# Sixty-eight elementwise operations moved from GpSimd to VectorE, and new figures in the planner that lays out a decoder layer

## The chip, the cores and the metric

The kernel runs on one core of one Trainium2 chip. A core has five engines with a queue of instructions each: TensorE (PE in the profile; PEld is its weight load), VectorE (DVE), ScalarE (ACT), GpSimd (POOL) and SyncE (SP, which here issues all DMAs). The metric is the device time of one execution in microseconds (us); the time before is the median of three runs.

## The reference

The reference computes one decoder layer in float32 for a sequence of 2048 tokens of width 1024. The input is normed and projected once to 59 blocks of 128 columns; the projection is cut into three branches, each of which has its own gate:

```python
h = rms_norm(x, norm_g[l])
p = h @ w_in[l]
y_a = rwkv7_mix(p_r, p_k, p_v, p_w, p_a, ...) * jax.nn.silu(z_a)
y_b = sliding_window_sink_attn(p_q, p_sk, p_sv, positions, ...) * jax.nn.silu(z_b)
y_c = memory_cross_attn(p_xq, mem, ...) * jax.nn.silu(z_c)
merged = (gates[:, :, 0] * (y_a @ w_proj_a[l]) + gates[:, :, 1] * (y_b @ w_proj_b[l])
          + gates[:, :, 2] * (y_c @ w_proj_c[l]))
x = x + (merged @ w_out[l])
```

Branch A is a recurrence over time with a state of 64x64 for each of 8 heads (`rwkv7_scan`). Branch B is attention over a sliding window of 128 tokens, branch C attention into 256 memory tokens.

## The kernel before

**Tiling.** The sequence is worked in four blocks of 512 tokens (`sb` from 0 to 3 in `build`). Within a block, features stand on the 128 partitions and the 512 tokens along the free axis.

**Dense products.** A float32 operand is cut into a high and a low part (type float32r), and a dense product is three matmuls, high by high, high by low and low by high (`gemm3`, L401, L402, L403; in the output projection L1036, L1037, L1038). The high part is a copy on ScalarE, the low part a subtraction. For the outputs of the branches this is `split_y`: ScalarE's copy at L829, the subtraction at L830, on GpSimd. It runs 48 times, 12 in each block of tokens. The keys of the memory are split in the same way at L547 (4 times).

**Weight blocks.** `wblock` brings 128 rows by 512 columns of a weight. In the first block of tokens it loads the raw block (tile `wraw`, L382), makes the high part on ScalarE (L383) and the low part on VectorE (L384) in a tile `whl`, and stores `whl` to memory (L387, tiles `k`). In the later three blocks it loads `whl` from there (L379). There are three buffers of each.

**The recurrence.** `rwkv_pair` works a pair of heads in 8 chunks of 64 tokens, one after the other. A chunk is a chain between TensorE and VectorE of three links: two matmuls at L749 give a product that VectorE copies to `W` (L760); two at L767 read `W`, and VectorE copies the result into `Z` (L773, L774); two at L777 read `Z`, and VectorE makes the next state (L784, twice), which L749 of the next chunk reads. There are 16 pairs, so 128 chunks. At L652, on GpSimd, r is multiplied by k for the bonus term, once for each pair. L678 to L680 are a loop of 31 steps on VectorE that inverts small triangles ahead of the chain. TensorE fills the time between links with dense matmuls of other branches.

**The other branches.** `swa_pair` (window attention) scales probabilities on VectorE (L983), transposes them on TensorE (L987), copies them on ScalarE (L989) and multiplies them by the values (L992). `merge` multiplies the branches by their output weights and gates (L1003, L1015, L1018, L1019).

**What sets the order.** The program is written by generators that are woven together, and then laid out anew. `steps` makes one step of each instruction, with the steps it depends on, a cost (`cost_PE`, `cost_DVE` and so on: how long the engine is busy, and when the result is there) and a rank, its number in the program. `lay_out` then goes through a clock of its own: for each engine it keeps the steps whose inputs are there by its reckoning, takes the engine that can start first, and on it the ready step of lowest rank (on TensorE with a preference for staying in one tile shape). A result of another engine is seen `LAT` ns after its reckoned end. A step that opens a tile waits until a buffer of that tag is free; buffers go in program order. `order` nails the result down as the order of every engine's queue. The small roots and powers of the norms (`rpow`, L366 to L370) stay on GpSimd in both kernels.

Of the kernel before, what the change touches and what calls it, by code (L numbers as in the profile page):

```python
# [9 lines left out]
F32 = mybir.dt.float32  # L10
# [4 lines left out]
ALU = mybir.AluOpType  # L15
# [24 lines left out]

LAT = {"PE": 55, "DVE": 45, "ACT": 35, "POOL": 80, "SP": 30}
NAMES = {mybir.EngineType.PE: "PE", mybir.EngineType.DVE: "DVE", mybir.EngineType.Activation: "ACT",
         mybir.EngineType.Pool: "POOL", mybir.EngineType.SP: "SP"}

# [1 line left out]
class Step:  # L48
# [32 lines left out]
    def cost_PE(self):  # L81
        out, mov, w = self.writes[0], *self.reads[:2]
        n = self.n(out)
        self.tile = tuple(128 if r[3][0][1] > 64 else 64 if r[3][0][1] > 32 else 32 for r in (mov, out))
        self.dense = mov[5] == F32R
        if self.dense:
            self.busy = 12 + 0.424 * n
        elif self.ins.is_transpose:
            self.busy = 108 if self.tile[0] == 128 else 55
        elif self.tile[1] == 128:  # L90
            self.busy = 223 + max(0, n - 128) * 1.7 if self.tile[0] == 128 else 223 + max(0, n - 128) * 0.8
        else:
            self.busy = max(58, 0.86 * n)
        self.dur = self.busy + 160

    def cost_ACT(self):
        r = self.reads[0]
# [13 lines left out]
        self.busy = self.dur + 80  # L111

    def cost_SP(self):
        self.dur, self.busy = 3300, 330


def steps(instructions, manual):

    out, masks, seen, byname, opener = [], {}, {}, {}, {}
    for ins in instructions:  # L120
        if isinstance(ins, mybir.BassTilePoolBoundary):
            continue
        s = Step(ins, masks)
        for rs, w in ((s.reads, False), (s.writes, True)):
            for name, parts, words, _, psum, _ in rs:
                s.before |= {q for q, w2, p2, m2 in seen.get(name, ()) if (w or w2 or psum) and q is not s and p2 & parts and m2 & words}
        for name, parts, words, *_ in s.reads:
            seen.setdefault(name, []).append((s, False, parts, words))
        for name, parts, words, *_ in s.writes:
            old = seen.setdefault(name, [])  # L130
            old[:] = [x for x in old if x[0] is s or x[2] & ~parts or x[3] & ~words] + [(s, True, parts, words)]
        s.before |= {byname[x] for x in manual.get(ins.name, ())}
        s.before |= {opener.setdefault(r[0], s) for r in s.writes + s.reads} - {s}
        for b in s.before:
            b.after.append(s)
        byname[ins.name] = s
        s.rank = len(out)
        out.append(s)
    return out

# [8 lines left out]
def lay_out(tc, todo):  # L149

    metas = {tag: meta.bufs for p in tc.info.pools if p.space != bass.MemoryType.DRAM for tag, meta in p.tag_meta.items()}
    source = {t.name: t.source_name for t in tc.info.tiles}
    tags = {tag: Tag(b) for tag, b in metas.items()}
    users, opened = {}, set()
    for s in todo:
        for name in {r[0] for r in s.reads + s.writes}:
            users.setdefault(name, []).append(s)
        for r in s.writes:
            if source[r[0]] in tags and r[0] not in opened:
                opened.add(r[0])  # L160
                s.opens.append(r[0])
                tags[source[r[0]]].queue.append(r[0])
    left = {name: len(u) for name, u in users.items()}
    heads = {tag: 0 for tag in tags}
    clock = {e: 0.0 for e in NAMES.values()}
    ready, parked = {e: {} for e in clock}, set()
    orders = {e: [] for e in clock}
    missing = {s: len(s.before) for s in todo}

    def seen_by(s, b):  # L170

        if b.eng == s.eng:
            return 0 if s.eng == "PE" else b.end + 30
        return b.end + LAT[s.eng]

    def room(s):

        at = 0.0
        for name in s.opens:
            t = tags[source[name]]  # L180
            if t.queue[heads[source[name]]] != name or not t.free:
                return None
            old = t.free[0]
            if old:
                at = max([at] + [seen_by(s, b) for b in last[old].values()])
        return at

    def offer(s):
        at = room(s)
        if at is None:  # L190
            parked.add(s)
            ready[s.eng].pop(s, None)
        else:
            parked.discard(s)
            ready[s.eng][s] = max([at] + [seen_by(s, b) for b in s.before])

    last = {name: {} for name in users}
    for s in todo:
        if not missing[s]:
            offer(s)  # L200
    tile, fp32 = (128, 128), False
    for _ in todo:
        best = None
        for e, rs in ready.items():
            if rs:
                at = max(clock[e], min(rs.values()))
                if best is None or at < best[0]:
                    best = at, e
        at, e = best
        can = [s for s, t in ready[e].items() if t <= at]  # L210
        s = min(can, key=lambda s: s.rank)
        if e == "PE":
            if tile != (128, 128) and s.tile != tile:
                s = min(can, key=lambda s: (s.tile != tile, s.rank))
            if s.tile != tile:
                at += 95
            if s.dense and fp32:
                clock[e] = at + 95
            else:
                clock[e] = at  # L220
            tile, fp32 = s.tile, not s.dense
            clock[e] += s.busy
        else:
            clock[e] = at + s.busy
        s.end = at + s.dur
        del ready[e][s]
        orders[e].append(s)
        again = set()
        for name in s.opens:
            tag = source[name]  # L230
            tags[tag].free.pop(0)
            heads[tag] += 1
            again.add(tag)
        for name in {r[0] for r in s.reads + s.writes}:
            if e not in last[name] or last[name][e].end < s.end:
                last[name][e] = s
            left[name] -= 1
            if not left[name] and source[name] in tags:
                tags[source[name]].free.append(name)
                again.add(source[name])  # L240
        for a in s.after:
            missing[a] -= 1
            if not missing[a]:
                offer(a)
        if again:
            for a in [a for rs in (parked, *ready.values()) for a in rs if any(source[n] in again for n in a.opens)]:
                offer(a)
    return orders
# [11 lines left out]
def build(tc, A, nsb=4):  # L260
    nc = tc.nc
    es = ExitStack()
    V, S, G, PE = nc.vector, nc.scalar, nc.gpsimd, nc.tensor
# [24 lines left out]
    def s_ps():  # L288
        return ps.tile([128, 512], F32, name="as_", bufs=2)
# [4 lines left out]
    manual = {}  # L294
# [158 lines left out]
    def bcast_T(out, st, nh, ntile):  # L453

        w = 128 // nh
        for i in range(ntile):
            rep = xp.tile([128, nh, w], F32, name="rep", bufs=2)
            V.tensor_copy(rep, st[:, i * nh:(i + 1) * nh].unsqueeze(2).to_broadcast([128, nh, w]))
            PE.transpose(out[:, i * 128:(i + 1) * 128], rep.rearrange("p a b -> p (a b)"), ident)
# [50 lines left out]
    KmH = cp.tile([128, 4, M], F32R, name="KmH")  # L510
    KmL = cp.tile([128, 4, M], F32R, name="KmL")
# [5 lines left out]
    def mem_kv():  # L517
# [23 lines left out]
        def scaled(h):  # L541
            kg = kgs[h][1]
            bc = s_ps()
            bcast_T(bc, sts[h], 1, 2)
            V.tensor_tensor(kg, kg, bc[:, :M], op=ALU.mult)
            S.activation(KmH[:, h], kg, AF.Copy)
            G.tensor_tensor(KmL[:, h], kg, KmH[:, h].bitcast(F32), op=ALU.subtract)  # L547

        o = [o_ps(), s_ps()]
        for h in range(6):  # L550
# [49 lines left out]
    def rwkv_pair(p, sb, hT, lwla, yas):  # L600
        kp = proj(B_K + p, hT)
        k = shift(kp, B_K + p, pcol("mu_k", p), dcol("omu_k", p), sb, "rk_")
# [46 lines left out]
        r = shift(rpj, B_R + p, pcol("mu_r", p), dcol("omu_r", p), sb, "rr_")  # L649
        for Q, h in ((QE, EV), (QO, OD)):  # L650
            V.tensor_tensor(Q[h, :, C:], chunks(r)[h], Pt[h, :, 1:], op=ALU.mult)
        G.tensor_tensor(r, r, k, op=ALU.mult)  # L652

        yield 12

# [19 lines left out]
        for s in range(31):  # L675
            n = 31 - s
# [68 lines left out]
        for c in range(NC_):  # L745
# [15 lines left out]
            SP = rp.tile([128, C], F32, name="SP", bufs=2)  # L761
# [64 lines left out]
    def split_y(y, yh, yl, br, j, sb):  # L826
        a = yp.tile([128, TB], F32R, name="yh")
        b = yp.tile([128, TB], F32R, name="yl")
        S.activation(a, y, AF.Copy)  # L829
        G.tensor_tensor(b, y, a.bitcast(F32), op=ALU.subtract)  # L830
        yh.append(a)
        yl.append(b)

# [346 lines left out]
```

## Time and profile before

| | us |
|---|---|
| median of 3 runs (2529.36 to 2537.97) | 2534.09 |
| the profiled execution | 2550.03 |
| its span, first to last instruction | 2548.2 |
| PE busy in the span | 2450.9 |
| DVE busy | 1546.8 |
| ACT busy | 893.2 |
| POOL busy | 202.2 |

The profile is of one execution. "Idle before" and the view of waits tell how long an engine stood with nothing running and whose event ended it; a wait of PEld is one of the weight load, which runs ahead of the matmul and may stand idle while PE works. The granted clock is the share of full speed that TensorE got; it is 1.0 or 0.5 in each stretch of the record. The times of one float32 matmul are those of two passes in the record, and an ordinary float32 matmul counts as two records.

### The profile page before, as it was taken

How to read it: one execution, taken by the hardware profiler on the slowest of the kernel's cores; microseconds unless marked ns; L12 is line 12 of the kernel's file. 1: busy time of each engine (PE TensorE's matmuls, PEld its weight loads, DVE VectorE, ACT ScalarE, POOL GpSimd, SP SyncE). 2: the span in 40 equal slices, each digit the busy share in tenths (PEclk: the TensorE clock that was granted, in tenths of full speed). 3: DMA queues.
4: the chain of work that ended last, by engine and by line, in shares of the span. 5: the costliest groups of instructions: out<-in, count | busy, mean ns of one | idle time of the engine just before them, and what ended most of it. 6: DMA issues, size and time to landing. Idle time of an engine off the chain costs nothing.

```text
span 2548.2 us, 39384 instructions
## 1 busy us (share of the span) xinstructions
PE 2450.9 (96%) x14496; PEld 1877.5 (74%) x14496; DVE 1546.8 (61%) x4962; ACT 893.2 (35%) x1957; POOL 202.2 (8%) x220
## 2 busy tenths in 40 slices
PE   6999999899999999999999999999999999999999
PEld 5676767678877777677777777767777777777777
DVE  6778876843666956636437685744553777573632
ACT  5445544433324343412223443331231334342120
POOL 1111101100001100100001100010000110000000
PEclk8899999999999999999999999989999999999999
DMA  5344446468842434244573333425466333433546
GB/s 172 133 167 154 171 164 221 159 230 291 304 163 93 150 109 140 93 161 157 178 248 124 104 124 125 149 83 174 141 220 210 100 135 118 141 116 130 176 136 228
DMA packets 132527, 407.37 MB, mean 160 GB/s; under 512 B 15344, under 2 KB 15728, under 8 KB 132336
## 3 DMA queue, kind: packets, MB, share of 16 engines
q1 hardware_dynamic: 132336, 404.86, 46.9%
q8 instruction: 115, 1.88, 0.3%
q14 instruction: 76, 0.62, 0.1%
HBM read 313.58 MB, written 91.23 MB: 159 GB/s over the span
## 4 chain that ended last, share of the span: by engine, by line
PE 73%; DVE 13%; DMA 6%; ACT 5%; issue 2%; SPq 1%; POOL 0%; DVEq 0%; ACTq 0%
PE mm L401 18%; PE mm L403 18%; PE mm L402 17%; DMA whl<-k 3%; PE oo L992 1%; PE rw L777 1%; PE rw L749 1%; PE rw L767 1%; PE oo L881 1%; DVE whl L384 1%; PE rw L662 1%; DVE g L983 1%; ACT g L972 1%; DVE ibc L678 1%; PE mm L1036 1%
## 5 line engine op out<-in xcount | busy, mean ns | idle before, releaser
L401 PE MATMUL mm<-hH,whl 128*128 128x512 f32 x1888 | 773.6, 410 | 13.6 <-DMA whl<-k 10.8
L403 PE MATMUL mm<-hH,whl 128*128 128x512 f32 x1888 | 766.1, 406 | 6.2 <-DVE whl L384 6.0
L402 PE MATMUL mm<-hL,whl 128*128 128x512 f32 x1888 | 762.7, 404 | 0.0
L401 PEld LDWEIGHTS mm<-hH,whl 128*128 128x128 f32 x1888 | 359.8, 191 | 103.4 <-issue 12.5
L403 PEld LDWEIGHTS mm<-hH,whl 128*128 128x128 f32 x1888 | 359.5, 190 | 84.0 <-DVE whl L384 7.6
L402 PEld LDWEIGHTS mm<-hL,whl 128*128 128x128 f32 x1888 | 360.0, 191 | 70.8 <-issue 1.4
L384 DVE TENSOR_TENSOR whl<-wraw,whl 128x512 fp32r<-128x512 f32 x174 | 123.7, 712 | 90.6 <-ACT whl L383 89.8
L383 ACT ACTIVATE whl<-wraw 128x512 fp32r<-128x512 f32 x174 | 109.0, 628 | 149.6 <-PE mm L403 86.5
L763 ACT ACTIVATE SP<-Z,Pt 64x64 f32<-64x64 f32 x256 | 88.5, 346 | 193.3 <-DVE Z L784 189.6
L679 DVE TENSOR_TENSOR ibc<-ibc,Yi 128x248 f32<-128x248 f32 (+30 forms) x496 | 150.4, 303 | 7.5
L1003 ACT ACTIVATE g<-mm 128x512 f32<-128x512 f32 x96 | 57.2, 596 | 273.6 <-PE mm L403 273.4
L401 PE MATMUL mm<-yh,whl 128*128 128x512 f32 x384 | 150.9, 393 | 2.2 <-DVE carry L590 2.2
L678 DVE STREAM_SHUFFLE ibc<-Nc 128x248 f32<-128x248 f32 (+30 forms) x496 | 151.7, 310 | 0.0
L402 PE MATMUL mm<-yl,whl 128*128 128x512 f32 x384 | 150.5, 392 | 0.0
L403 PE MATMUL mm<-yh,whl 128*128 128x512 f32 x384 | 150.2, 391 | 0.0
L680 DVE TENSOR_TENSOR Yi<-Yi,ibc 128x248 f32<-128x248 f32 (+30 forms) x496 | 149.1, 301 | 0.8
L1018 DVE SCALAR_TENSOR_TENSOR g<-g,mm 128x512 f32<-128x512 f32 x64 | 43.9, 685 | 124.9 <-PE mm L403 103.8
L784 DVE SCALAR_TENSOR_TENSOR Z<-rw,Pt,SP 64x64 f32<-64x64 f32 x224 | 63.4, 283 | 59.4 <-PE rw L777 55.6
L972 ACT ACTIVATE g<-g,mxs,st 128x256 f32<-128x256 f32 (+1 forms) x128 | 74.4, 583 | 61.5 <-DVE mxs L965 61.4
L760 DVE COPY W<-rw 128x64 f32<-128x64 f32 x128 | 28.6, 223 | 110.1 <-PE rw L749 109.7
L401 PEld LDWEIGHTS mm<-yh,whl 128*128 128x128 f32 x384 | 72.5, 189 | 17.6 <-DVE carry L590 2.4
L402 PEld LDWEIGHTS mm<-yl,whl 128*128 128x128 f32 x384 | 72.5, 189 | 14.9
(1737 smaller groups left out, 3979.1 us busy)
## 6 DMA issues: line engine op xcount, KB each, us to landing
whl<-k SPq DMA_DIRECT2D x474, 512.0 KB, 3.3
k<-whl SPq DMA_DIRECT2D x158, 512.0 KB, 3.2
wraw<-in_w_in SPq DMA_DIRECT2D x118, 256.0 KB, 3.8
g<-in_x SPq DMA_DIRECT2D x36, 256.0 KB, 5.5
out<-g SPq DMA_DIRECT2D x32, 256.0 KB, 3.5
rt<-in_x SPq DMA_DIRECT2D x28, 256.0 KB, 4.6
wraw<-in_w_proj SPq DMA_DIRECT2D x24, 256.0 KB, 3.5
wraw<-in_w_out SPq DMA_DIRECT2D x16, 256.0 KB, 4.1
```

What stands on the lines that cost most here:

```text
L383: S.activation(w[:, 0], raw, AF.Copy)
L384: V.tensor_tensor(w[:, 1], raw, w[:, 0].bitcast(F32), op=ALU.subtract)
L401: PE.matmul(out, lh, rh, start=i == 0, stop=False)
L402: PE.matmul(out, lh, rl, start=False, stop=False)
L403: PE.matmul(out, ll, rh, start=False, stop=i == n - 1)
L678: V.stream_shuffle(bc[:, :, :n], Nc[:, :, s + 1:], [s] * 32)
L679: V.tensor_tensor(bc[:, :, :n], bc[:, :, :n], Y[:, :, s:s + 1].to_broadcast([128, NC_, n]), op=ALU.mult)
L680: V.tensor_tensor(Y[:, :, s + 1:], Y[:, :, s + 1:], bc[:, :, :n], op=ALU.add)
L763: S.activation(SP[h], Z[h, e, c], AF.Copy, scale=Pt[h, c, C:C + 1])
L784: upd = V.scalar_tensor_tensor(to, pS[h], Pt[h, c, C:C + 1], SP[h], op0=ALU.mult, op1=ALU.add)
L972: S.activation(prs[b][:, i, m0:], prs[b][:, i, m0:], AF.Exp, scale=r2[:, b, i:i + 1], bias=mx[:, b, i:i + 1], accum_out=mx[:, b, 2 + i:3 + i])
L1003: S.activation(t, gp, AF.Tanh, scale=0.5)
```

## The change

Three kinds of lines change. First, the 48 subtractions of `split_y`, the 4 of the memory keys and the 16 products of r and k are given to VectorE. Second, the planner's figures: results of TensorE are seen by other engines 200 ns after their end instead of 55, a matmul's own result takes at least 270 ns, a dense matmul is 2 ns longer, some float32 shapes are costed otherwise, the clock of TensorE is advanced differently where shapes change, and a DMA takes 3800 ns instead of 3300. Third, every step that writes a tile `whl` or `wraw` (the loads of weights, the copy L383 and the subtraction L384) gets a rank that is 1000 lower, so that among ready steps of an engine it is taken before others.

```diff
-LAT = {"PE": 55, "DVE": 45, "ACT": 35, "POOL": 80, "SP": 30}
+LAT = {"PE": 200, "DVE": 45, "ACT": 35, "POOL": 80, "SP": 30}
...
-            self.busy = 12 + 0.424 * n
+            self.busy = 14 + 0.424 * n
...
-            self.busy = 223 + max(0, n - 128) * 1.7 if self.tile[0] == 128 else 223 + max(0, n - 128) * 0.8
+            self.busy = 223 + max(0, n - 128) * 1.7 if self.tile[0] == 128 else 175 + max(0, n - 128) * 0.9
...
-        self.dur = self.busy + 160
+        self.dur = max(270, self.busy + 160)
...
-        self.dur, self.busy = 3300, 330
-
-
-def steps(instructions, manual):
+        self.dur, self.busy = 3800, 380
+
+
+def steps(instructions, manual, ahead=1000):
...
-        s.rank = len(out)
+        s.rank = len(out) - ahead * any(n.startswith(a) for n, *_ in s.writes for a in ("whl", "wraw"))
...
+            clock[e] = at + s.busy
             if s.dense and fp32:
-                clock[e] = at + 95
-            else:
-                clock[e] = at
+                clock[e] += 95
+            elif s.tile != tile and s.tile[1] < 128:
+                clock[e] += 49
             tile, fp32 = s.tile, not s.dense
-            clock[e] += s.busy
...
-            G.tensor_tensor(KmL[:, h], kg, KmH[:, h].bitcast(F32), op=ALU.subtract)
+            V.tensor_tensor(KmL[:, h], kg, KmH[:, h].bitcast(F32), op=ALU.subtract)
...
-        G.tensor_tensor(r, r, k, op=ALU.mult)
+        V.tensor_tensor(r, r, k, op=ALU.mult)
...
-        G.tensor_tensor(b, y, a.bitcast(F32), op=ALU.subtract)
+        V.tensor_tensor(b, y, a.bitcast(F32), op=ALU.subtract)
```

The first place is on TensorE, in one chunk of the recurrence in the second block of tokens. The rows go from L749 to L777; rows of `mm` are dense matmuls, the numbers behind names are those of buffers. Before:

```order
L749 MATMUL rw_11717<-Z_11608,QE_11057 64x64
L749 MATMUL rw_11717<-Z_11608,QO_11058 64x64
L756 MATMUL yps_11672<-Z_11608,QE_11057 64x64
L756 MATMUL yps_11672<-Z_11608,QO_11058 64x64
L402 MATMUL mm_11739<-hL_6530,whl_11742 128x512
L767 MATMUL rw_11727<-W_11722,Tt_156 64x64 x2
L737 MATMUL yps_11672<-Z_11608,AB_11203 64x64 x2
L403 MATMUL mm_11739<-hH_6529,whl_11742 128x512
L401 MATMUL mm_11739<-hH_6529,whl_11742 128x512
L777 MATMUL rw_11734<-Z_11608,bkT_11561 64x64 x2
```

And with the change:

```order
L749 MATMUL rw_11717<-Z_11608,QE_11057 64x64
L749 MATMUL rw_11717<-Z_11608,QO_11058 64x64
L756 MATMUL yps_11672<-Z_11608,QE_11057 64x64
L756 MATMUL yps_11672<-Z_11608,QO_11058 64x64
L402 MATMUL mm_11739<-hL_6530,whl_11742 128x512
L403 MATMUL mm_11739<-hH_6529,whl_11742 128x512
L767 MATMUL rw_11727<-W_11722,Tt_156 64x64 x2
L737 MATMUL yps_11672<-Z_11608,AB_11203 64x64 x2
L401 MATMUL mm_11739<-hH_6529,whl_11742 128x512
L402 MATMUL mm_11739<-hL_6530,whl_11742 128x512
L403 MATMUL mm_11739<-hH_6529,whl_11742 128x512
L777 MATMUL rw_11734<-Z_11608,bkT_11561 64x64 x2
```

Two dense matmuls instead of one stand between L749 and L767, and three instead of two between L767 and L777. Over the 128 chunks the commonest number goes from one (92 chunks) to two (87) in the first of these links, from two (79) to three (73) in the second, and from three (51 of 112) to four (66) between L777 and the next L749. The dense matmuls are the same in number; the changes from a run of dense matmuls to float32 ones and back go from 702 runs to 719.

The second place is on VectorE, in the middle of the second block of tokens, where the probabilities of one head pair are scaled (L983) while the recurrence of another goes on. Before:

```order
L976 RECIPROCAL dns_10497<-dns_10497 128x8
L983 TENSOR_SCALAR g2_10393<-g2_10393,dns_10497 128x256 x2
L983 TENSOR_SCALAR g2_10394<-g2_10394,dns_10497 128x256 x2
L983 TENSOR_SCALAR g2_10409<-g2_10409,dns_10497 128x256 x2
L983 TENSOR_SCALAR g2_10410<-g2_10410,dns_10497 128x256 x2
L1015 SCALAR_TENSOR_TENSOR mB_10493<-g2_10478,mm_10480 128x512
L760 COPY W_10516<-rw_10511 128x64
```

With the change:

```order
L983 TENSOR_SCALAR g2_10409<-g2_10409,dns_10497 128x256 x2
L983 TENSOR_SCALAR g2_10410<-g2_10410,dns_10497 128x256 x2
L830 TENSOR_TENSOR yl_9117<-g2_9112,yh_9116 128x512
L830 TENSOR_TENSOR yl_9620<-g2_9615,yh_9619 128x512
L830 TENSOR_TENSOR yl_10145<-g2_10140,yh_10144 128x512
L1015 SCALAR_TENSOR_TENSOR mB_10493<-g2_10478,mm_10480 128x512
L760 COPY W_10516<-rw_10511 128x64
```

Three of the moved subtractions now stand between the scaling and the copy to `W`. On TensorE, three dense matmuls now stand between the transposes L987 and the L767 that reads this `W`; before, none did. Of the 68 moved operations, 14 have a step of the recurrence among the next three rows of VectorE's queue.

The third place is SyncE's queue in the first block of tokens. Before:

```order
L387 DMA k120_6056<-whl_6051 128x1024
L382 DMA wraw_6100<-in_w_in 128x512
L387 DMA k121_6063<-whl_6058 128x1024
L382 DMA wraw_6134<-in_w_in 128x512
L387 DMA k122_6097<-whl_6092 128x1024
```

With the change:

```order
L382 DMA wraw_6100<-in_w_in 128x512
L387 DMA k120_6056<-whl_6051 128x1024
L382 DMA wraw_6134<-in_w_in 128x512
L387 DMA k121_6063<-whl_6058 128x1024
L382 DMA wraw_6141<-in_w_in 128x512
```

The load of a raw block now stands ahead of the store of an earlier finished one, instead of behind it. At the program's start the first three raw blocks stand ahead of the rows of x, on SyncE as on ScalarE and VectorE; before, they stood behind them.

## The prediction

> **What bounds the kernel now.** I read the page's busy times first, then the waits of PE, of PEld, then the granted clock, then timelines of places where PE stood.
>
> ```profile
> PE 2450.9 (96%) x14496; PEld 1877.5 (74%) x14496; DVE 1546.8 (61%) x4962; ACT 893.2 (35%) x1957; POOL 202.2 (8%) x220
> PE rw L432 <- DVE rt L427: 16.1, 4, 13.9
> PE mm L401 <- DMA whl<-k: 10.8, 12, 2.5
> PE rw L767 <- DVE W L760: 9.2, 6, 2.6
> PE mm L403 <- DVE whl L384: 6.0, 2, 5.3
> PE mm L1036 <- DMA whl<-k: 3.5, 5, 1.0
> PEld rw L777 <- issue: 42.8, 102, 1.6
> PEld rw L767 <- DVE W L760: 33.8, 91, 2.8
> core 0: 2548.2 us, clock 0.979
> ```
>
> TensorE sets the time: it is busy 2450.9 of 2548.2 us, and the change neither adds nor removes a matmul. What can move is the idle 97.3 us, the waits that the busy time hides (a matmul's modelled end covers the short ones), and the clock: a mean of 0.979 means that 0.021 x 2548.2 = 53.5 us were lost at half speed. The first wait of 13.9 us is the start, before the first row of x is normed.
>
> The second thing to see is a place in which three engines stand in each other's way. Here is VectorE, then GpSimd, then TensorE, in the second block of tokens:
>
> ```profile
> 1051.61 5.25 DVE L983 TENSOR_SCALAR g<-g,dns 128x256 f32<-128x256 f32 x8
> 1056.89 0.69 DVE L1015 SCALAR_TENSOR_TENSOR mB<-g,mm 128x512 f32<-128x512 f32 x1
> 1057.50 0.22 DVE L760 COPY W<-rw 128x64 f32<-128x64 f32 x1
> 1052.61 3.84 POOL L830 TENSOR_TENSOR yl<-g,yh 128x512 fp32r<-128x512 f32 x3 [14.44 <-ACT yh L829]
> 1054.70 0.49 PE L987 MATMUL as__10571<-c_ident,g 128*128 128x128 f32 x3
> 1057.77 0.37 PE L767 MATMUL rw<-W,Tt 64*64 64x64 f32 x2 [2.58 <-DVE W L760]
> L983 DVE TENSOR_SCALAR g<-g,dns x128: 268/345/1428, 305.1 to 2287.5; 128x256 f32<-128x256 f32 x120, 128x128 f32<-128x128 f32 x8
> 463.72 1.50 DVE L679 TENSOR_TENSOR ibc<-ibc,Yi 128x208 f32<-128x208 f32 x1
> 463.09 0.36 DVE L680 TENSOR_TENSOR Yi<-Yi,ibc 128x216 f32<-128x216 f32 x1
> ```
>
> Eight scalings take 5.25 us, though the median of one is 345 ns, so 2.8 us for eight; the extra 2.5 us fall exactly where GpSimd runs three subtractions (3.84 us). VectorE is held up by GpSimd's long operations: a product at 463.72 takes 1.50 us where its larger neighbour took 0.36. `W` comes late, and TensorE stands 2.58 us. What follows is worse than the wait. Stretches of the granted clock:
>
> ```profile
> 471.00:481.30 10.30, 9.21 (x22) 6.76 (x23) 8.16 (x40) 5.79 (x19) 0.00 (x0) 0.52 0.62 229
> 1058.00:1068.20 10.20, 10.20 (x83) 7.17 (x79) 2.38 (x10) 3.17 (x7) 0.29 (x1) 0.51 0.01 2
> 1676.00:1696.50 20.50, 20.50 (x114) 13.54 (x114) 3.88 (x16) 3.90 (x10) 0.00 (x0) 0.51 0.07 26
> 2290.00:2303.70 13.70, 13.70 (x93) 8.63 (x89) 3.22 (x13) 3.27 (x8) 0.00 (x0) 0.50 0.00 1
> sum 75.10, PE 73.03 PEld 51.32 DVE 29.79 ACT 16.95 POOL 2.79; mean PE 8.11 PEld 5.70 DVE 3.31 ACT 1.88 POOL 0.31
> ```
>
> The seventh figure behind the stretch's length is the clock. The stretch at 471 follows the 5.3 us wait of L403, the other three follow the same place in the second, third and fourth block of tokens. The sum is over the nine half-clock stretches after the first 300 us.
>
> **The change, term by term.** All gains are TensorE time, since nothing else sets the end.
>
> *Moved operations.* GpSimd loses these, and VectorE gets them at the price of like operations of its own (both inputs in on-chip memory, 128x512):
>
> ```profile
> 0.00:2548.20 2548.20, 63.44 (x48) 0.98 0.47 160
> 0.00:2548.20 2548.20, 21.84 (x16) 0.98 0.47 160
> L1027 DVE TENSOR_TENSOR mB<-mB,g 128x512 fp32r<-128x512 f32 x32 | 22.1, 691 | 16.4 <-ACT g L1025 16.1
> L633 DVE TENSOR_TENSOR rt<-rt,Pt 128x512 f32<-128x512 f32 x16 | 11.1, 691 | 4.0 <-ACT Pt L614 3.3 <-PE rw L805 0.5
> ```
>
> The first row is L830 on GpSimd, the second L652. On VectorE they cost (48 + 16) x 0.691 = 44.2 us, the four half-size ones at L547 some 2 us more, so 46. Against it stand the hold-ups: if each us of GpSimd cost VectorE what it did above, 2.5 / 3.84 = 0.65, then 0.65 x 85.3 = 55 us would go; where VectorE is idle none does. I take 30. VectorE then is busy some 1563 of 2548 us, and the 39% in which it is idle now hide the rest. Without that cover the 16 us would be paid in full.
>
> What TensorE gets back: in the changed order three subtractions stand ahead of this `W`, so it comes after 8 x 0.345 + 3 x 0.69 + 0.69 = 5.5 us from 1051.61, 0.4 us earlier than now; and three dense matmuls of 0.23 us now stand ahead of L767. Of the 2.58 us, 1.1 go at least, all at most, where VectorE overlaps neighbours (L1015 started `W` 0.61 us after itself, not 0.69). I take 1.4, three times: 4. Of L403's 6.0 us I take 3, since the hold-up seen there in one row is 1.1 us and the subtraction L384 is also ranked ahead. **7 us**, from 4 to 14.
>
> *Results of TensorE taken later.* One chunk of the recurrence, TensorE and then VectorE's copy:
>
> ```profile
> 1207.11 0.39 PE L401 MATMUL mm<-hH,whl 128*128 128x512 f32 x1
> 1207.46 0.34 PE L777 MATMUL rw<-Z,bkT 128*64 128x64 f32 x4
> 1207.73 0.50 PE L402 MATMUL mm<-hL,whl 128*128 128x512 f32 x1
> 1208.07 0.40 PE L403 MATMUL mm<-hH,whl 128*128 128x512 f32 x1
> 1208.30 0.39 PE L401 MATMUL mm<-hH,whl 128*128 128x512 f32 x1
> 1208.62 0.27 PE L749 MATMUL rw<-Z,QE 128*64 128x64 f32 x1
> 1208.63 0.27 PE L749 MATMUL rw<-Z,QO 128*64 128x64 f32 x1
> 1209.00 0.50 PE L402 MATMUL mm<-hL,whl 128*128 128x512 f32 x1
> 1209.43 0.27 PE L767 MATMUL rw<-W,Tt 64*64 64x64 f32 x2
> 1209.00 0.22 DVE L760 COPY W<-rw 128x64 f32<-128x64 f32 x1 [0.57 <-PE rw L749]
> ```
>
> A dense matmul follows another after 0.23 us, and a small one follows it after 0.32 (L749) if it waits for nothing. L767 follows after 0.43: it waits 0.11 us for `W`, which no view shows as idle PE. From L749's second matmul to `W` are 0.37 us, where the old planner reckons 55 + 160 + 58 = 273 ns and the new one 270 + 200 = 470. So the old one believed that one dense matmul fills the link, and the new one puts two. The second dense matmul has to be done anyway; the 0.11 us go. Weight loads of L767 waited for `W` 91 times: 91 x 0.11 = 10 us. L777 follows its dense matmul after 0.35, so 0.03 us, 102 times: 3 us. **13 us**; none if the new queue only moves the waits elsewhere; 21 if each of the 102 waits were as long as L767's.
>
> *The rest of PE's idle time* is 97.3 - 13.9 - 9.2 - 6.0 - 14.3 (the two rows of weights) = 53.9 us, in many small waits for VectorE and ScalarE after a TensorE result, which the old planner put 145 ns too early. A third of it: **18 us**, from 0 to two thirds, 36.
>
> *Weights first.* SyncE issues four loads of x at the start in this time:
>
> ```profile
> 1.17 1.84 SPq L316 DMA_DIRECT2D rt<-in_x  x4
> ```
>
> The two rows of DMA waits are 14.3 us. Those loads are of the later blocks, which wait for a buffer that TensorE frees, and a rank frees none; in the first block the raw load now passes the store ahead of it on SP, and the copy and the subtraction pass other work. Who is behind: the store, which nobody needs before the next block of tokens, and at the start the rows of x, behind three raw blocks on SP and on ACT; x is on the path there. Three issues of 1.84 / 4 = 0.46 us are 1.4 us later, against a shorter queue behind it. **5 us**, from 0 to 14.
>
> *The clock.* Half of 75.1 us, 37, was lost in the nine stretches. The four shown (54.7 us, so 27 lost) follow holds that term one shortens: I take 16 of them, not all, since about 1 us of wait may stay at three places. Of the other 10 I take 4. **20 us**, from 0 to 37.
>
> [...]
>
> *What it costs.* Seventeen more changes from dense to float32 work and back: 0.09 us to get in (0.32 - 0.23), 0.11 for the second dense matmul after (L402 to L403 in the chunk is 0.34 instead of 0.23), and a little to get out, so 0.25 in all, an estimate: 17 x 0.25 = **4 us**. Fourteen of the 68 moved operations stand within three rows ahead of a step of the recurrence; at 0.69 us each that is 10 us if every one is waited for, nothing if none: **3 us**.
>
> Sum: 7 + 13 + 18 + 5 + 20 - 7 = 56 us, so 2550.0 - 56 = 2494 for a profiled execution. The profiled one was 15.9 us longer than the median of the runs; on the median it is 2534.1 - 56 = **2478 us**.
>
> **Rivals.**
>
> *The clock stays low.* The half-clock stretches lie over thin work (83 matmul records in 10.2 us at 1058), and may come from that, not from the wait. For it: the stretch at 1676 lasts 20.5 us, far longer than any wait. Against it: wait and drop stand together four times. Then 56 - 20 = 36: 2498 us.
>
> *Everything goes at once*: terms near their upper ends, since the planner's error was everywhere and shorter waits keep the clock. 14 + 18 + 30 + 10 + 30 - 7 = 95, less 10 for what a new order always opens: 2449.
>
> *An exchange.* The new queue removes waits of one kind and opens as many of another (14 moved operations at 0.69, new waits for weights): 2534, give or take 8. For it: the longest waits for weights (2.5 us) and for L384 (5.3 us) are single ones, such as any order may have. Against: the wait of 0.11 us repeats 91 times, and the count of dense matmuls in the links closes it.
>
> *VectorE takes GpSimd's place*, the slower side. Every moved operation stands whole in a queue in which `W` and `Z` wait: 0.69 - 0.23 (the spare dense matmul) = 0.46 us a time, 64 times 29 us; threes in a row (16 groups) drop the clock for at least 3.4 us, 1.7 lost each, 27 us. With 4 for changes, against 13 + 5 + 18 gained: 24 us slower, 2558. It decides from about 40 of the 64 in front of a waiting step; the order shows 14.
>
> **How the numbers follow.** The forecast 0.55, the low clock 0.22, everything 0.10, an exchange 0.07, VectorE 0.06. Within 0.3% of 2534.1 is 2526.5 to 2541.7, about what a measurement of this kernel can tell from no change. Faster has the first three, 0.87; same 0.07; slower 0.06. The range of 2448 to 2524 holds the forecast with its terms at either end, the low clock and half of the large gain; it leaves out the other half, the exchange and the slow case, 0.18.
>
> **What would show it.** The eight L983 should take under 3 us, and no L679 more than 0.5. The PEld waits of L767 for `W` should fall from 91 times to under 20, and L767 should follow its dense matmul after 0.32. PE's idle time should fall to some 65 us and the mean clock rise to 0.985 or more. VectorE's busy time should rise by less than 30 us. I am wrong if L767 waits behind L830 on VectorE, if the clock stays at 0.979, or if new waits for `whl` appear in the three later blocks.

## The result and the profile after

The changed kernel takes 2502.93 us, the median of four runs (2499.77 to 2506.89). The kernel before took 2535.14 beside it. The ratio is 0.9877, with a 95% interval of 0.9853 to 0.990: faster by 32 us, where 56 were forecast. The profiled execution took 2506.89 us.

These are the rows of after that answer to those shown of before: first the page's busy times, then the waits (engine, line, what it waited for: total us, times, longest), then the span and mean clock.

```profile
PE 2423.5 (97%) x14496; PEld 1849.8 (74%) x14496; DVE 1554.1 (62%) x5030; ACT 890.5 (36%) x1957; POOL 111.3 (4%) x152
```

```profile
PE rw L432 <- DMA c_ident<-in_ident: 12.2, 1, 12.2
PE mm L401 <- DVE carry L590: 10.4, 5, 3.3
PE mm L401 <- DMA whl<-k: 9.7, 10, 3.0
PE as__1022 L459 <- DVE rep L458: 4.6, 1, 4.6
PE mm L1036 <- DMA whl<-k: 3.8, 7, 1.5
PE rw L767 <- DVE W L760: 1.7, 4, 0.5
PE mm L403 <- DVE whl L384: 0.8, 1, 0.8
PEld rw L777 <- issue: 37.6, 92, 1.6
PEld rw L767 <- DVE W L760: 26.1, 66, 1.0
```

```profile
core 0: 2504.9 us, clock 0.993
```

The two waits on which the prediction dwelt are nearly gone: `W` from 9.2 to 1.7 us and the wait of L403 from 6.0 to 0.8. But PE's idle time only falls from 97.3 to 2504.9 - 2423.5 = 81.4 us, because others have opened: for `carry` 10.4 us instead of 2.2, and a single 4.6 us for `rep`. The largest difference is the clock: 0.979 meant 53.5 us lost, 0.993 means 17.5. Of the 43.1 us between the two profiled executions, some 36 are clock.

Here is the place of three engines in after: the timeline (start, us, engine, line), a window around it (length, busy us of PE, PEld, DVE, ACT, POOL, then the clock) and the groups of two lines (ns: least, median, longest):

```profile
1042.63 0.88 DVE L983 TENSOR_SCALAR g<-g,dns 128x256 f32<-128x256 f32 x3
1043.75 0.34 DVE L983 TENSOR_SCALAR g<-g,dns 128x256 f32<-128x256 f32 x1
1044.42 1.14 DVE L983 TENSOR_SCALAR g<-g,dns 128x256 f32<-128x256 f32 x4
1045.48 0.68 DVE L830 TENSOR_TENSOR yl<-g,yh 128x512 fp32r<-128x512 f32 x1
1046.48 1.29 DVE L830 TENSOR_TENSOR yl<-g,yh 128x512 fp32r<-128x512 f32 x2 [0.31 <-ACT yh L829]
1048.41 0.22 DVE L760 COPY W<-rw 128x64 f32<-128x64 f32 x1
1048.68 0.27 PE L767 MATMUL rw<-W,Tt 64*64 64x64 f32 x2 [0.53 <-DVE W L760]
```

```profile
1036.00:1056.00 20.00, 19.07 (x165) 13.08 (x162) 10.26 (x35) 12.09 (x34) 0.30 (x1) 1.00 0.25 81
```

```profile
L983 DVE TENSOR_SCALAR g<-g,dns x128: 278/345/358, 309.3 to 2248.0; 128x256 f32<-128x256 f32 x120, 128x128 f32<-128x128 f32 x8
L679 DVE TENSOR_TENSOR ibc<-ibc,Yi x496: 165/284/411, 67.5 to 2371.5; 128x248 f32<-128x248 f32 x6, 128x224 f32<-128x224 f32 x6, 128x200 f32<-128x200 f32 x6, 128x176 f32<-128x176 f32 x6
```

The eight scalings take 0.88 + 0.34 + 1.14 = 2.36 us, not 5.25. The three subtractions now stand in front of `W`, as the order had it, and TensorE waits 0.53 us instead of 2.58. The window around it is at full clock (1.00), where before had 10.2 us at 0.51. The longest L983 is 358 ns instead of 1428.

A chunk of the recurrence in after, again from the timeline:

```profile
1036.16 0.50 PE L402 MATMUL mm<-hL,whl 128*128 128x512 f32 x1
1036.16 0.22 DVE L760 COPY W<-rw 128x64 f32<-128x64 f32 x1 [0.78 <-PE rw L749]
1036.50 0.40 PE L403 MATMUL mm<-hH,whl 128*128 128x512 f32 x1
1036.83 0.33 PE L767 MATMUL rw<-W,Tt 64*64 64x64 f32 x4
```

Two dense matmuls stand in the link, and L767 follows the second after 0.33 us, the step of a matmul that waits for nothing (0.32 for the L749 at 1208.62 us in before).

### The profile page after: what moved, and what is told of

Same layout as the page of the kernel before. It is cut to its first block, busy times and chain, and to the rows that moved or that the text cites. A ratio compares the mean times of both kernels' runs of the same rounds, so it can differ in the third digit from the quotient of the medians.

```text
span 2504.9 us, 39317 instructions
## 1 busy us (share of the span) xinstructions
PE 2423.5 (97%) x14496; PEld 1849.8 (74%) x14496; DVE 1554.1 (62%) x5030; ACT 890.5 (36%) x1957; POOL 111.3 (4%) x152
## 4 chain that ended last, share of the span: by engine, by line
PE 69%; DVE 8%; DMA 5%; ACT 4%; issue 1%; SPq 0%; POOL 0%; ACTq 0%; DVEq 0%
PE mm L401 17%; PE mm L403 16%; PE mm L402 16%; DMA whl<-k 3%; PE oo L992 1%; PE rw L662 1%; PE rw L749 1%; PE rw L767 1%; PE rw L777 1%; PE oo L881 1%; DMA rt<-in_x 1%; PE mm L1036 1%; PE mm L1037 1%; PE mm L1038 1%; DMA out<-g 1%
## 5 line engine op out<-in xcount | busy, mean ns | idle before, releaser
L401 PE MATMUL mm<-hH,whl 128*128 128x512 f32 x1888 | 771.8, 409 | 23.7 <-DMA whl<-k 9.7
L403 PE MATMUL mm<-hH,whl 128*128 128x512 f32 x1888 | 759.0, 402 | 0.8 <-DVE whl L384 0.8
L401 PEld LDWEIGHTS mm<-hH,whl 128*128 128x128 f32 x1888 | 357.3, 189 | 112.1 <-issue 24.7
L403 PEld LDWEIGHTS mm<-hH,whl 128*128 128x128 f32 x1888 | 357.9, 190 | 75.5 <-issue 2.9
L383 ACT ACTIVATE whl<-wraw 128x512 fp32r<-128x512 f32 x174 | 109.3, 629 | 230.0 <-PE mm L403 157.3
L384 DVE TENSOR_TENSOR whl<-wraw,whl 128x512 fp32r<-128x512 f32 x174 | 119.7, 689 | 102.8 <-ACT whl L383 101.0
L401 PE MATMUL mm<-yh,whl 128*128 128x512 f32 x384 | 150.6, 392 | 0.0
L403 PE MATMUL mm<-yh,whl 128*128 128x512 f32 x384 | 150.5, 392 | 0.0
L679 DVE TENSOR_TENSOR ibc<-ibc,Yi 128x248 f32<-128x248 f32 (+30 forms) x496 | 142.5, 287 | 7.0
L680 DVE TENSOR_TENSOR Yi<-Yi,ibc 128x248 f32<-128x248 f32 (+30 forms) x496 | 139.5, 281 | 0.9
L1003 ACT ACTIVATE g<-mm 128x512 f32<-128x512 f32 x96 | 57.0, 594 | 215.7 <-PE mm L403 215.3
L401 PEld LDWEIGHTS mm<-yh,whl 128*128 128x128 f32 x384 | 72.1, 188 | 15.2 <-issue 0.2
```

The costliest lines, as they stand in the source:

```text
L383: S.activation(w[:, 0], raw, AF.Copy)
L384: V.tensor_tensor(w[:, 1], raw, w[:, 0].bitcast(F32), op=ALU.subtract)
L401: PE.matmul(out, lh, rh, start=i == 0, stop=False)
L403: PE.matmul(out, ll, rh, start=False, stop=i == n - 1)
L679: V.tensor_tensor(bc[:, :, :n], bc[:, :, :n], Y[:, :, s:s + 1].to_broadcast([128, NC_, n]), op=ALU.mult)
L680: V.tensor_tensor(Y[:, :, s + 1:], Y[:, :, s + 1:], bc[:, :, :n], op=ALU.add)
```

## The experiments

**The theories.** A, mine: long operations of GpSimd hold VectorE up, so `W` comes late in the second to fourth blocks of tokens, and the clock halves behind it. B: the planner's figures, by which TensorE takes results later, so that more dense work stands in the links. C: the weights taken first. The rival on the clock: it halves because the work there is thin, whatever the wait.

To read the runs I split each time in two. What the clock cost is put at (1 - mean granted clock) x span, as if TensorE were busy in all of it; the rest is about what the execution would take at full clock. The clock is given to 0.001, which is 1.3 us, and its record begins only 15 to 28 us into the span (16.7 in before, 27.1 in the change), so a half clock before that is counted in the rest: a split is good to some 3 us. The medians of all timed runs, each taken by itself, so that a row need not add up to the us:

| kernel | runs | us | lost at half clock | rest | ratio to before |
|---|---|---|---|---|---|
| before, beside all experiments | 53 | 2537.3 | 33 | 2503 | |
| e_memset | 6 | 2517.0 | 18 | 2497 | 0.9919 (0.9898 to 0.9939) |
| e_moves: moves alone | 6 | 2515.7 | 26 | 2490 | 0.9913 (0.9894 to 0.9932) |
| e_planner: planner's figures alone | 6 | 2509.2 | 20 | 2489 | 0.9889 (0.9867 to 0.991) |
| e_weights: rank ahead alone | 12 | 2529.2 | 24 | 2504 | 0.9967 (0.995 to 0.9984) |
| e_lat: one planner figure | 12 | 2527.8 | 28 | 2499 | 0.9965 (0.995 to 0.998) |
| e_no_weights: moves, planner | 6 | 2501.3 | 25 | 2478 | 0.9854 (0.983 to 0.9878) |
| e_no_moves: planner, ahead | 6 | 2501.9 | 13 | 2490 | 0.986 (0.9837 to 0.9883) |
| e_no_planner: moves, ahead | 6 | 2502.7 | 11 | 2492 | 0.9864 (0.9838 to 0.989) |
| the change: all three | 4 | 2502.9 | 16 | 2487 | 0.9877 (0.9853 to 0.990) |
| e_late_all | 5 | 2489.8 | 22 | 2467 | 0.9813 (0.9798 to 0.9828) |
| e_late_all0 | 4 | 2491.8 | 21 | 2472 | 0.9819 (0.9805 to 0.9833) |
| e_ahead150 | 4 | 2498.2 | 15 | 2483 | 0.9844 (0.983 to 0.9857) |
| e_late_ahead150 | 5 | 2493.2 | 20 | 2473 | 0.9823 (0.9799 to 0.9847) |

**Is it the hold-up, and does the clock follow the wait?** The kernel before, with the queues of TensorE, VectorE, ScalarE and SyncE as they were. GpSimd's 48 subtractions are replaced by fills with zero in the same places; this leaves out the low parts of the branches' outputs.

```diff
-        S.activation(a, y, AF.Copy)
-        G.tensor_tensor(b, y, a.bitcast(F32), op=ALU.subtract)
+        act = S.activation(a, y, AF.Copy)
+        behind(G.memset(b.bitcast(F32), 0.0), act, True)
```

> The kernel before, with GpSimd's 48 subtractions of the branch outputs replaced by a memset of the same tile to zero (so the low parts of the branch outputs are left out of the result). The queues of TensorE, VectorE, ScalarE and SyncE are the same as before, row for row; only what GpSimd reads is gone. Theory A (GpSimd's long reads hold VectorE up, TensorE then stands and its clock drops): the three waits of 2.58 us of L767 for W fall under 0.3, the eight L983 take under 3 us, the half-clock stretches at the same three places go, the mean clock rises from 0.979 to about 0.99, and the time is 2508 to 2518. Rival (the clock drops because the work there is thin, not because of the wait): the waits go, some 10 us are saved, 2523 to 2528, and the three half-clock stretches stay.

Measured: 2517.0 us, 20 less than before. The timeline of the same place, and windows over the matmuls that before ran at half clock, there and in the next two blocks:

```profile
1047.10 3.29 DVE L983 TENSOR_SCALAR g<-g,dns 128x256 f32<-128x256 f32 x8
1048.09 0.62 POOL L830 MEMSET yl<- 128x512 f32 x1 [14.42 <-ACT yh L829]
1051.03 0.22 DVE L760 COPY W<-rw 128x64 f32<-128x64 f32 x1
1051.30 0.27 PE L767 MATMUL rw<-W,Tt 64*64 64x64 f32 x2 [0.60 <-DVE W L760]
```

```profile
1051.50:1058.30 6.80, 6.80 (x87) 4.81 (x84) 2.47 (x10) 3.18 (x7) 0.29 (x1) 1.00 0.08 32
1659.10:1671.70 12.60, 12.54 (x115) 8.74 (x115) 3.98 (x16) 3.96 (x10) 0.00 (x0) 1.00 0.10 29
2262.70:2271.50 8.80, 8.74 (x96) 5.68 (x93) 3.26 (x13) 3.27 (x8) 0.00 (x0) 1.00 0.01 2
```

With the same instructions in the same order on VectorE and TensorE, the eight scalings take 3.29 us instead of 5.25 and the wait 0.60 instead of 2.58 (0.61 in the next two blocks). That is a little more than the 3 and 0.3 us expected, since a fill still holds a scaling up (the longest L983 takes 768 ns, the median one 348). All three stretches are at full clock, over the same thin work. This shows theory A, the clock included, and rules out thin work alone as the cause there. By the medians the clock's share falls by 15 us and the rest by 6.

**Each part alone.** e_moves has only the 68 operations on VectorE, e_planner only the planner's figures, e_weights only the rank ahead, each with its lines of the change and nothing else, for instance:

```diff
-        s.rank = len(out)
+        s.rank = len(out) - ahead * any(n.startswith(a) for n, *_ in s.writes for a in ("whl", "wraw"))
```

> The kernel before with only the 68 operations moved to VectorE; the planner's figures and ranks are the old ones. Theory A: most of the gain, 2508 to 2518, since VectorE is no longer held up, less what the three subtractions ahead of W cost. Theory B (the gain is the planner's later results): 2530 to 2540.

> The kernel before with only the planner's figures changed; operations stay on GpSimd, ranks as before. Theory A: at most 12 us faster from the links of the recurrence, 2522 to 2532, with the half-clock stretches behind GpSimd's subtractions still there. Theory B: 2503 to 2515.

> The kernel before with only the steps of weight blocks ranked 1000 ahead. Theories A and B: within 8 us of before, 2527 to 2540, with the waits for the weights of the later blocks unchanged and the start no earlier. Theory C (weights first is what saves): 2515 or less.

Measured: 2515.7, 2509.2 and 2529.2, that is 22, 28 and 8 us less than before. Theory A has the first and the third, but gave the planner 12 us at most; 28 is in theory B's range. Together the parts give 58, where the change gains 32 to 34: they share something. Why the planner gains without taking anything from GpSimd shows in its timeline at the same place:

```profile
1045.42 0.34 DVE L983 TENSOR_SCALAR g<-g,dns 128x256 f32<-128x256 f32 x1
1046.09 1.15 DVE L983 TENSOR_SCALAR g<-g,dns 128x256 f32<-128x256 f32 x4
1047.16 3.75 POOL L830 TENSOR_TENSOR yl<-g,yh 128x512 fp32r<-128x512 f32 x3 [15.42 <-ACT yh L829]
1047.85 0.69 DVE L1015 SCALAR_TENSOR_TENSOR mB<-g,mm 128x512 f32<-128x512 f32 x1 [0.61 <-PE mm L403]
1048.45 0.22 DVE L760 COPY W<-rw 128x64 f32<-128x64 f32 x1
1049.07 0.27 PE L767 MATMUL rw<-W,Tt 64*64 64x64 f32 x2
```

GpSimd still does its three subtractions, but the scalings are all but done when they start, and the two operations of VectorE beside them run at their usual 0.69 and 0.22 us. L767 waits for nothing. So either edit ends the same loss, one by removing GpSimd's work, the other by moving VectorE's ahead of it. The rank ahead does neither; its rows still read as before:

```profile
L983 DVE TENSOR_SCALAR g<-g,dns x128: 270/349/1422, 303.0 to 2268.1; 128x256 f32<-128x256 f32 x120, 128x128 f32<-128x128 f32 x8
```

```profile
PE rw L767 <- DVE W L760: 8.2, 4, 2.6
```

What the rank ahead does end is the longest wait of before behind its start, 5.3 us of L403 for the subtraction L384. With the moves alone this row is 7.7 us in all, with the rank alone 0.4 (e_moves, then e_weights):

```profile
PE mm L403 <- DVE whl L384: 7.7, 3, 5.5
PE mm L403 <- DVE whl L384: 0.4, 1, 0.4
```

In its place e_weights has a wait of 5.2 us for `g` of L983, at L987.

**Two parts at a time.** The change with one part undone each.

```diff
-def steps(instructions, manual, ahead=1000):
+def steps(instructions, manual, ahead=0):
```

(e_no_weights; e_no_moves gives the 68 operations back to GpSimd, e_no_planner has the old figures.)

> The change without the rank ahead: the 68 moved operations and the planner's new figures stand, the weight steps keep their rank. Theory S (both edits end the same loss: the three 2.6 us waits at g, Z, W of L983 to L767 and the half-clock stretches behind them, so that what the one takes the other can't take again): 2507, between 2500 and 2512, clock 0.991 to 0.994, about what the planner's figures gave alone (2509). Theory D (different losses, gains add up): 2537 less 22 less 28, 2487. If the rank ahead costs at the start (the first wait of TensorE, for c_ident, 12.2 us): faster than the change by up to 5.

> The change with the 68 operations left on GpSimd: the planner's figures and the rank ahead stand. Theory S: 2506, between 2500 and 2511, since the planner's figures alone took the g and W place out of the hold-ups' way (L830's hold-ups of 21 us fell elsewhere); the moves are worth at most 6 us on top. Theory D: 2503 plus the moves' 22, 2525. The longest L983 stays under 0.5 us by S, and is 1.4 us again somewhere by D.

> The moves and the rank ahead with the planner's old figures. Theory S: the moves alone gave 2516, the rank ahead 8 us alone; it brought less full-clock idle time at L1036 and L401 for whl, which the moves don't touch, so most of it should add: 2509, between 2505 and 2516. Theory D: 2507. Where the planner's later results have a share of their own (my term B, 13 us in the forecast), this stays 8 to 13 us over the change: 2511 to 2516.

Measured: 2501.3, 2501.9 and 2502.7. Any two of the parts give what all three give. Theory S held for the first two, at the lower end of its ranges, and theory D missed them by 14 and 23 us. e_no_planner came out below either and level with the change, where my term B was to leave it 8 to 13 us behind. The split says why. At full clock the moves are worth 11 to 14 us, added to before, to the planner's figures or to the rank ahead (2503 to 2490, 2489 to 2478, 2504 to 2492), and the planner's figures 12 to 14 in the same way (2503 to 2489, 2490 to 2478, 2504 to 2490). These two nearly add: 14 and 14 alone, 26 together. What they share is the clock, 7 and 13 us alone and 8 together (33 to 26, 20 and 25). So theory S came out in its number, but its reason holds for the clock more than for the rest. The rank ahead is worth nothing at full clock by itself (2503 to 2504), and costs 10 on top of both (2478 to 2487). What it brings is clock: 7 to 15 us less is lost with it than without. The same stretch of time, from 260 to 345 us, without and with it (e_no_weights, then the change):

```profile
260.00:345.00 85.00, 74.94 (x382) 58.21 (x382) 68.49 (x238) 34.16 (x69) 6.59 (x6) 0.90 0.46 159
```

```profile
260.00:345.00 85.00, 80.49 (x437) 61.48 (x436) 72.32 (x238) 36.92 (x75) 6.98 (x6) 0.96 0.57 195
```

And what it costs, from the timeline of the change at 162 us:

```profile
161.97 0.69 DVE L384 TENSOR_TENSOR whl<-wraw,whl 128x512 fp32r<-128x512 f32 x1
163.97 0.67 DVE L646 TENSOR_TENSOR BK<-rk__1554,rt 64x512 f32<-64x512 f32 x1
164.57 0.68 DVE L384 TENSOR_TENSOR whl<-wraw,whl 128x512 fp32r<-128x512 f32 x1
166.11 0.15 DVE L590 COPY carry<-mm 128x1 f32<-128x1 f32 x1
166.41 0.47 PE L401 MATMUL mm<-hH,whl 128*128 128x512 f32 x1 [3.28 <-DVE carry L590]
```

The copy to `carry` takes 0.15 us and is the last reader of a result `mm`; until it has run, L401 has no place to write. It stands behind two subtractions of weights, among others, that were ranked ahead. TensorE waits 3.28 us. e_no_weights has no wait for `carry` there.

**One figure of the planner.** What the figure means has to be read in the code that uses it:

```python
    def seen_by(s, b):

        if b.eng == s.eng:
            return 0 if s.eng == "PE" else b.end + 30
        return b.end + LAT[s.eng]
```

Here `b` makes the result and `s` takes it, and the figure is that of the engine that takes. So 55 and 200 are not how late other engines see TensorE's results, as the description of the change has it, but how long after the end of another engine's step TensorE is believed to start. In the chunk that the prediction shows, `W` ends at 1209.22 us and L767 starts at 1209.43, 0.21 us later. This run is the kernel before with that figure alone.

```diff
-LAT = {"PE": 55, "DVE": 45, "ACT": 35, "POOL": 80, "SP": 30}
+LAT = {"PE": 200, "DVE": 45, "ACT": 35, "POOL": 80, "SP": 30}
```

> The kernel before with one figure changed: TensorE takes a result at 200 in place of 55; prices, moves and ranks as before. If that figure is what the planner's part lives on (L767 placed later behind W): 2509 to 2515, longest L983 under 0.5 us, half-clock stretches after 1000 us gone. If the prices of fp32 beside dense matmuls and of SP's issues carry it: 2525 to 2537 with L983 at 1.4 us still.

Measured: 2527.8, a third of the planner's gain. The rows are mixed too:

```profile
L983 DVE TENSOR_SCALAR g<-g,dns x128: 270/347/1357, 310.3 to 2268.5; 128x256 f32<-128x256 f32 x120, 128x128 f32<-128x128 f32 x8
```

```profile
PE rw L767 <- DVE W L760: 3.7, 4, 1.0
```

The figure does shorten the link, but the scalings still stand beside GpSimd. For the matmuls at full clock I took from the trace by how much they started later than their usual distance from the matmul ahead of them allows (for L767 behind a dense one, 0.33 us). L767 behind a dense matmul was late by 11.2 us in all before, 3.8 with this figure alone and 2.4 after, so 7.4 us leave this link. PE's idle time all the same does not fall (2525.8 - 2427.5 = 98.3 us, against 97.3), because others open: the waits for `rep` grow from 5.2 to 9.9 us, those for `g` of L983 from 2.5 to 7.0. The other 18 us of the planner's gain come with its prices, or with where the new order happens to put the scalings; which of them, these runs don't tell.

**Can the rest be had?** After's new waits are for steps of VectorE (`carry`, `rep`), which take results of other engines themselves. By the planner VectorE does so 45 ns after their end, and ScalarE 35; here they too are given more.

```diff
-LAT = {"PE": 200, "DVE": 45, "ACT": 35, "POOL": 80, "SP": 30}
+LAT = {"PE": 200, "DVE": 150, "ACT": 120, "POOL": 80, "SP": 30}
```

This on the change is e_late_all; with `ahead=0` as well, e_late_all0; the change with only `ahead=150`, e_ahead150; the later results and `ahead=150`, e_late_ahead150.

> The change, with VectorE and ScalarE also taking results later in the layout: 150 in place of 45 and 120 in place of 35. Theory L (what is left of TensorE's idle time is made of results asked for too early, as VectorE's operands are: the new waits for carry, rep and g, 10.4 + 7.2 + 2.5 us, shrink by half): 2488 to 2496. Rival X (the layout only exchanges one wait for another, as the four versions between 2501 and 2503 suggest): 2503, give or take 6.

> The same later results for VectorE and ScalarE, without the rank ahead. Theory L: 2486 to 2494, since without the rank ahead the full-clock part was 10 us less. Rival X: 2501, give or take 6, with the half-clock stretches near 275 and 330 us still there (25 us of clock loss).

> The change with the weight steps 150 steps ahead, not 1000. If the rank ahead buys clock (the gaps at 272 to 331 us, which are waits for g L938 and carry L590 behind a late start) and pays with the waits of the first 200 us (c_ident, hL, rep, carry: 10 us at full clock), a short lead may keep most of the one without the other: 2493 to 2499. If the two belong together, or the lead's size doesn't matter: 2500 to 2504.

> The change with VectorE's and ScalarE's results also taken later (150 and 120) and the weight steps 150 steps ahead in place of 1000. If the two gains are of different places (later results: the waits of TensorE all along; the shorter lead: the stretches of half clock and the waits of the first 350 us), they add: 2490 less 4 to 5, 2483 to 2487. If the layout only exchanges here: 2488 to 2493.

Measured: 2489.8, 2491.8, 2498.2 and 2493.2. e_late_all is faster than both kernels: 13 us below the change (its slowest run, 2494.7, is below the change's fastest, 2499.8) and 1.9% below before (ratio 0.9798 to 0.9828). From its busy times and waits:

```profile
PE 2421.0 (97%) x14496; PEld 1854.8 (75%) x14496; DVE 1550.4 (62%) x5030; ACT 889.2 (36%) x1957; POOL 113.9 (5%) x152
```

```profile
PE mm L401 <- DMA whl<-k: 5.4, 12, 0.7
PE mm L401 <- DVE carry L590: 5.0, 2, 3.1
PE as__1022 L459 <- DVE rep L458: 3.8, 1, 3.8
PEld rw L767 <- DVE W L760: 5.7, 14, 0.5
```

PE has no wait for `W` any more, its weight loads wait for it 14 times instead of 66, and PE's idle time is 2487.7 - 2421.0 = 66.7 us. In the traces L767 starts 0.70 us after the last L749 in before, 0.93 in the change and 1.16 here (medians of the chunks at full clock): one dense matmul of 0.23 us more each time, and so more time for `W` to come. Of the three waits that the expectation named only `carry` halved; those for `rep` went from 7.2 to 8.5 us, those for `g` of L1003 from 2.5 to 3.9. What fell beside it are the two rows of waits for weights, from 13.5 to 6.9. So the time came out as theory L had it, and its reason in part. The rank ahead again makes no difference (2489.8 against 2491.8). A short lead gains 5 us on the change, as its expectation had it, but not on e_late_all, where the fourth run was to give 2483 to 2487: there the layout only exchanges.

## Why the prediction was right, and where it was too large

The direction, the cause and the order of the rivals held; 2502.9 lies in the range. The sum was 24 us too large. Step by step:

- **The clock, 20 us: right in size, with some luck.** 17 by the medians of the table (33 to 16), 36 by the two profiled executions, since the profiled one of before lost more than its like (53 us against a median of 33). The term was worked out from that one execution and taken off the median. The three stretches of half clock at `W` are gone, and e_memset shows that they came from the wait: gaps of 0.60 us in place of 2.58 left none there. I did not see that the rank ahead would bring clock too. Most of what the change still loses lies in the first 600 us, 27 of 37 us at half clock in its trace.
- **Moved operations, 7 us: too small.** 11 to 14 at full clock. VectorE's busy time rose by 7.3 us (46 added, so 39 of hold-ups gone, where I took 30). The wait of L767 kept 0.53 us where I left 1.2. L403 lost 5.2 of 6.0 where I took 3, but that is not the moves' doing: it goes wherever the rank ahead is (0.4 to 0.8 us in all seven runs that have it) and stays with the moves alone (7.7) and with moves and planner (8.9). The 3 us set against the sum, for moved operations ahead of a step of the recurrence, are not to be seen.
- **Results taken later (13) and the rest of PE's idle time (18): these failed.** After 4 us for changes of shape they were to give 27; the planner's figures give 12 to 14 added to before or to one other part, and 5 added to both (2492 to 2487). The first I derived from the wrong half of the link: by `seen_by` the 145 ns lie between VectorE's `W` and L767, not between L749 and `W`. The link as a whole becomes as much longer as I reckoned, by 52 + 145 = 197 ns, and L767 and L777 were late by 11.2 + 7.7 us before and 2.4 + 5.5 after, 11 us less, against 13. (The 102 waits of L777 that I priced end with "issue" in the profile, so nothing there shows that they were for `Z`.) But e_no_planner still has the link delays of before (11.0 and 6.0) and takes the time of the change. The third of the other waits that I counted on top did not go: the same subtraction as in the prediction gives 81.4 - 12.2 - 1.7 - 0.8 - 13.5 = 53.2 us in the change, against 53.9. Some of these waits did close, for `QE` from 5.3 to 0.6 us and for `rt` of L608 from 4.4 to 2.3, but others opened: `carry` from 2.2 to 10.4, `rep` from 5.2 to 7.2. I wrote of an exchange as a rival of its own; in truth it was part of this case. Why the new order opens just these is not shown. e_late_all, where VectorE and ScalarE also take results later, gets 20 us more of the rest (2487 to 2467), and loses 6 more to the clock.
- **Weights first, 5 us: right alone, nothing in company.** The two rows of DMA waits fell from 14.3 to 13.5 us, so it is not through the loads. Added to the other two it ends the wait for L384 (8.9 to 0.8 us), doubles that for `carry` (5.3 to 10.4), costs 10 us at full clock and brings 9 of clock. I had named the subtraction L384 as "ranked ahead" and priced who stands behind it on SyncE, but not on VectorE, where the copy that frees TensorE's output stands.
- **The gauges.** The scalings, L679, the clock and VectorE's busy time came as foretold. PE's idle time came to 81, not 65, because of the exchange above. The count of weight loads that wait for `W` was a poor gauge: it fell only from 91 to 66, although L767 now follows after 0.33 us. A weight load may wait for its input while the matmuls ahead of it still run: in the change those of L767 wait 26.1 us for `W`, PE itself 1.7.
- **Rivals.** The clock did not stay low, and VectorE did not take GpSimd's place: the three subtractions do stand in front of `W`, which I had named as a sign of being wrong, but cost only 0.53 us there.

## What to carry to other kernels

When parts of a change act on one and the same stall, they share what it costs: look at each part's time with the others absent before adding terms, and split off the clock's share, to which one wait can add more than its own length (behind 2.58 us here came 10.2 us at a clock of 0.51) and which differs from one execution of a kernel to the next (mean clocks of before: 0.979 to 0.993). In a planner's table of delays, look up in the code whether a figure belongs to the engine that makes a result or to the one that takes it. To give one engine more time may only move the waits: here TensorE's figure alone gave 10 us, and giving VectorE and ScalarE more time as well brought 13 on top of the whole change. Before ranking work ahead, look on every engine that does it for the short steps that free another engine's buffers.

## What the hardware showed beside this

- **Which operations hold each other up.** With L830 on GpSimd, VectorE's scalings from and to on-chip memory took up to 1428 ns instead of 345 (median), and the products of L679 up to 1504, where none takes over 411 in the change. A zero fill of 0.53 us (median), which reads nothing, let them take up to 768. In e_planner a copy of TensorE's result (0.22 us) and L1015, which also reads one (0.69), ran beside three subtractions at their usual length. GpSimd's small powers (L370, at most 128x8, some 1.5 us) overlapped 44 of L679, L680 and L983 in before, and none of these took over 409 ns. What the longest scalings lose is less than one operation of GpSimd takes: 1428 - 345 = 1083 ns beside an L830 of 1.32 us (mean), 768 - 348 = 420 ns beside a fill of 0.53. Why L830 and a fill hold VectorE up and a small power, which also runs 1.5 us by the profile (whose spans on GpSimd are rough), does not, these runs don't show.
- **What the clock does.** In before the half-clock stretches behind `W` were 10.2, 20.5 and 13.7 us. The shortest in its record last 3.4 us, which is the length that the rival on VectorE was priced with:

```profile
1088.40:1091.80 3.40, 3.38 (x8) 2.71 (x9) 0.69 (x1) 0.00 (x0) 0.60 (x1) 0.51 0.07 27
```

In the change this wait was followed by one of 3.4 us (timeline, then windows):

```profile
1227.23 0.50 PE L401 MATMUL mm<-hH,whl 128*128 128x512 f32 x1 [1.94 <-DMA whl<-k]
```

```profile
1225.20:1227.40 2.20, 0.26 (x2) 0.17 (x2) 1.60 (x5) 2.13 (x4) 0.56 (x1) 1.00 0.94 347
1228.60:1232.00 3.40, 3.40 (x10) 2.62 (x9) 0.89 (x2) 1.35 (x3) 0.00 (x0) 0.50 0.06 20
```

The gap here was 1.94 us; gaps of 1.58 and 1.51 us in the same execution (at 656 and 1291 us) were followed by none, and neither was one of 2.27 at 480. So the length of the gap alone does not decide it. What does stays open.
